# A start offset per stage for the weight tiles that TensorE reads

## The chip, the cores and the metric

The kernel runs on 1 core of a Trainium2 chip. The metric is the device time of one execution in microseconds (us). The median of three runs of the kernel before is 1837.48 us (1835.64 to 1839.0).

## The reference

Two blocks follow each other on a sequence of 256 positions and 1024 channels, in float32. The first is a mixer of four branches (a gated linear recurrence, mean pools, a chunked linear attention, a short convolution), each branch projected and gated, then an MLP. The second block runs twice: a SwiGLU layer, a mixer of windowed attention and a wide depthwise convolution, and a second SwiGLU layer. What matters here are the large products, all of the form activation times weight:

```python
proj = jnp.einsum("btd,dp->btp", u, w_in[l])            # first block, 1024 -> 6656
hid = jnp.square(jax.nn.relu(jnp.einsum("btd,df->btf", u, w_up[l])))
m = jnp.einsum("btf,fd->btd", hid, w_down[l])
...
def swiglu_ffn(h, w_up, w_down):                        # second block, twice a layer, two layers
    a, b = jnp.split(h @ w_up, 2, axis=-1)
    return (jax.nn.silu(a) * b) @ w_down
...
z = h @ w_in + b_in                                     # second block's mixer
return (g_attn * y_attn + g_conv * y_conv) @ w_out
```

## The kernel before

Activations lie transposed, channels on the 128 partitions and the 256 positions along the free dimension. TensorE multiplies in fp32r, and each factor is split in two so that the product is accurate: a value is a high part (rounded to fp32r) and a low part (the rest). A product of a weight block and an activation block is three TensorE products into the same PSUM tile: high by high, high by low, low by high.

**The weights** come in pieces of 128 x 2048 floats (1 MB), 290 of them, in the order of a queue that `plan` fills. `weights` (lines 164 to 193) handles one piece: SyncE starts a DMA into a tile `raw` (a ring of two), ScalarE casts it into a tile `hi`, and then either VectorE subtracts `hi` from `raw` into a tile `lo` (`how == 0`), or, for half of the `qkv` pieces and all `gat` pieces (`how == 1`), ScalarE writes minus the high part to `lo` and a DMA from GpSimd's queue adds the weights on top. `hi` and `lo` are rings of three tiles of 8,192 bytes per partition. `self.ahead` keeps up to two pieces prepared ahead of the one in use.

**The products.** `mm_pair` (line 225) runs a piece: for 8 blocks `k` and 2 output halves `m` three products, 48 in all, each with a 128 x 128 block of the weights as the loaded (stationary) operand and 256 columns of activations as the streamed (moving) operand:

```python
three = [(h, H), (h, L), (lo, H)]
...
nc.tensor.matmul(pt[:, m], w[:, i, c], x[k], ...)
```

`mm_duo` (line 248) does the same for two pieces at once, and lines 669 to 673 for the attention's projection. In the `qkv` stage (lines 512 to 514) the operands change places: the activations are loaded, and 512 columns of weights are streamed. Here a product means one such load of 128 columns with the stream that follows it.

**The stages**, by the names of their weights in the queue, with pieces x products of a piece: `win` 26 x 48, `wbr` 4 x 48, `wout` 4 x 48, `wup` 16 x 48, `wdown` 16 x 48, and then for each layer 0 and 1 `ffn1u` 1056 products, `ffn1d` 528, `glu` 384, `qkv` 432 (of 512 columns), `gat` 384, `att` 96, `cpr` 192, `out` 192, `ffn2u` 1056, `ffn2d` 528.

**Where the operands lie.** Pools follow each other in SBUF: `raw`, `hi`, `lo`, small constants, then the activations. In the built program the three `hi` tiles start at bytes 32,896, 41,088 and 49,280 of a partition, the `lo` tiles at 57,472, 65,664 and 73,856. These are 128 bytes past a multiple of 256. The activations that TensorE reads with them are the tiles `xs0` to `xs3` (from 99,488) and `slot0` to `slot16` (from 115,872), each in a place of 4,096 bytes, and all of them start 160 bytes past a multiple of 256. A block of weights is a multiple of 512 bytes into its tile, a block of activations a multiple of 1,024. So in every fp32r product of the kernel the weights' address less the activations' is -32 modulo 256, in all stages alike.

The instruction order is what the tile framework makes of the program order, with a few stretches raised in priority; the change touches none of it.

Of the kernel before, what the change touches and what calls it, by code (L numbers as in the profile page):

```python
# [11 lines left out]
F32R = mybir.dt.float32r  # L12
# [5 lines left out]
P = 128  # L18
# [9 lines left out]
NL = 2  # L28
NEG = -1e30
CH = 2048  # L30

PERM = np.arange(NT).reshape(16, 4, 4).transpose(2, 1, 0).reshape(-1)

# [7 lines left out]
def _pairs(w):  # L41

    k, m = w.shape
    return w.reshape(k // P, P, m // 256, 256).transpose(2, 1, 0, 3).reshape(m // 256, P, -1)


def _duo(w):

    k, m2 = w.shape
    n = m2 // 256  # L50
    return w.reshape(k // P, P, 2, n, P).transpose(3, 1, 0, 2, 4).reshape(n, P, -1)


def _wide(w):

    k, m = w.shape
    return w.reshape(k // 512, 4, P, m // 512, 512).transpose(3, 0, 2, 1, 4).reshape(
        m // 512, k // 512, P, CH)

# [15 lines left out]
def layout2(A):  # L75

    W, prm = {}, Pack()
    for l in range(NL):
# [4 lines left out]
        wi = g("w_in")  # L83
        W[f"qkv{l}"] = _wide(wi[:, :4608]).reshape(18, P, CH)
        W[f"glu{l}"] = _duo(wi[:, 4608:6656])
        W[f"gat{l}"] = _duo(wi[:, 6656:])
        W[f"att{l}"] = _wide(g("w_attn_proj")).reshape(2, P, CH)
        W[f"cpr{l}"] = _pairs(g("w_conv_proj"))
# [40 lines left out]
class Builder:  # L129
# [27 lines left out]

    def plan(self, name, i, cols=CH, c0=0, how=0):

        self.queue.append((name, i, c0, cols, how))  # L160

    def weights(self, name, i, c0=0, first=None):
        key = (name, i, c0)
        while key not in self.ready or self.next_ < min(self.ready[key][2] + 1 + self.ahead, len(self.queue)):
            n, ii, cc, w, how = self.queue[self.next_]
            nc = self.nc
            r = self.p_raw.tile([P, CH], F32, name="raw")
            h = self.p_hi.tile([P, CH], F32R, name="hi")
            lo = self.p_lo.tile([P, CH], F32R, name="lo")
            if self.next_ < 2:  # L170
                for j in range(4):
                    c = slice(j * 512, (j + 1) * 512)
                    if self.next_ == 0:
                        first(j)
                    nc.sync.dma_start(r[:, c], self.d[n][ii, :, c])
                    nc.scalar.copy(h[:, c], r[:, c])  # L176
                    nc.vector.tensor_sub(lo[:, c], r[:, c], h[:, c].bitcast(F32))
                self.ready[n, ii, cc] = (h, lo, self.next_)
                self.next_ += 1
                continue  # L180
            nc.sync.dma_start(r[:, :w], self.d[n][ii, :, cc:cc + w])
            if how == 1:
                nc.scalar.mul(lo[:, :w], r[:, :w], -1.0)  # L183
                nc.gpsimd.dma_start(lo[:, :w], self.d[n][ii, :, cc:cc + w], accum_op=ALU.add)
            nc.scalar.copy(h[:, :w], r[:, :w])  # L185
            if how == 0:
                nc.vector.tensor_sub(lo[:, :w], r[:, :w], h[:, :w].bitcast(F32))  # L187
            self.ready[n, ii, cc] = (h, lo, self.next_)
            self.next_ += 1
        h, lo, _ = self.ready[key]  # L190
        return h, lo
# [1053 lines left out]
```

## Time and profile before

| what | value |
|---|---|
| median of three runs | 1837.48 us (1835.64 to 1839.0) |
| profiled execution, its own time | 1843.05 us |
| its span, first to last instruction | 1840.9 us |
| mean granted TensorE clock | 0.988 |
| TensorE busy with products | 1774.8 us (96%), 14048 products |
| VectorE / ScalarE busy | 1328.8 us (72%) / 921.1 us (50%) |
| share of the span on the chain that ended last | TensorE 68%, DMA 10%, VectorE 10%, ScalarE 5% |

The profile page gives busy times per engine, the chain of work that ended last, and groups of instructions by source line. Products overlap one another on TensorE (one lasts 280 ns, but the next begins some 117 ns after it), so a product's duration does not say what it costs: its pace, the time from one start to the next, does. A pace is read by counting the products in a stretch in which the engine never idles.

### The profile page before, as it was taken

The numbers are of one execution on the slowest core, as the hardware profiler recorded it, in microseconds if no ns is written. First come the engines' busy times: TensorE is split into PE (matmuls) and PEld (weight loads), VectorE is DVE, ScalarE is ACT, GpSimd is POOL, SyncE is SP. The second block draws the span as 40 slices with busy tenths as digits, with TensorE's granted clock in tenths as the row PEclk, the third lists the DMA queues.
The fourth block names the chain that finished last, engine by engine and source line by source line (L and its number), as shares of the span: only waits on it lengthen the run. The fifth ranks groups of instructions, "written<-read, shape, count | busy, mean of one in ns | idle before, by whom it ended". The sixth has DMA issues, their size and how long they took to land.

```text
span 1840.9 us, 32917 instructions
## 1 busy us (share of the span) xinstructions
PE 1774.8 (96%) x14048; PEld 1693.8 (92%) x14048; DVE 1328.8 (72%) x2038; ACT 921.1 (50%) x1041; POOL 45.7 (2%) x69
## 2 busy tenths in 40 slices
PE   8999989998999999989999999999999989999997
PEld 7989889998999987778999999999997778999997
DVE  7986877546665698978776656765698988776653
ACT  5354454434444455466654445444455566654442
POOL 0000000000100000000000000100000000000000
PEclk9999999999999999989999999999999999999998
DMA  7526445554555579886455545555569986455552
GB/s 286 168 97 218 161 139 192 184 194 139 193 184 181 186 226 252 268 211 170 141 184 192 194 168 199 191 184 180 188 199 279 256 229 175 138 183 185 187 184 86
DMA packets 53570, 348.47 MB, mean 189 GB/s; under 512 B 6192, under 2 KB 6320, under 8 KB 14256
## 3 DMA queue, kind: packets, MB, share of 16 engines
q1 hardware_dynamic: 47376, 308.66, 47.4%
q0 software_dynamic: 4896, 35.65, 10.3%
q8 instruction: 110, 1.80, 0.4%
q10 hardware_dynamic: 1152, 2.06, 0.3%
q14 instruction: 36, 0.29, 0.0%
HBM read 345.30 MB, written 1.05 MB: 188 GB/s over the span
## 4 chain that ended last, share of the span: by engine, by line
PE 68%; DMA 10%; DVE 10%; ACT 5%; issue 4%; POOL 0%; ACTq 0%; DVEq 0%; POOLq 0%
PE mm L225 60%; DMA raw<-qkv 5%; DVE lo L187 4%; ACT hi L185 3%; DMA raw<-gat 2%; PE y L596 1%; DMA lo<-qkv 1%; PE mm L248 1%; PE tr L588 1%; PE pc L316 1%; PE pc L306 1%; PE sc L571 1%; DMA raw<-win 1%; DMA raw<-out 1%; PE mm L513 0%
## 5 line engine op out<-in xcount | busy, mean ns | idle before, releaser
L225 PE MATMUL mm<-xs,hi 128*128 128x256 f32 x5440 | 967.8, 282 | 10.6 <-ACT hi L176 5.9
L225 PEld LDWEIGHTS mm<-xs,hi 128*128 128x128 f32 x5440 | 825.9, 189 | 18.4 <-ACT hi L176 5.9
L187 DVE TENSOR_TENSOR lo<-raw,hi 128x2048 fp32r<-128x2048 f32 (+1 forms) x254 | 574.0, 2260 | 317.2 <-ACT hi L185 316.3
L185 ACT CAST hi<-raw 128x2048 fp32r<-128x2048 f32 (+1 forms) x288 | 541.9, 1885 | 422.8 <-PE mm L225 343.1
L225 PE MATMUL mm<-xs,lo 128*128 128x256 f32 x2720 | 739.1, 282 | 7.4 <-DVE lo L187 3.7
L225 PEld LDWEIGHTS mm<-xs,lo 128*128 128x128 f32 x2720 | 501.6, 189 | 11.6 <-DVE lo L187 4.5
L225 PE MATMUL mm<-slot,hi 128*128 128x256 f32 x2304 | 401.3, 280 | 3.0 <-DVE slot L939 2.4
L225 PEld LDWEIGHTS mm<-slot,hi 128*128 128x128 f32 x2304 | 346.1, 188 | 4.0 <-DVE slot L939 2.8
L225 PE MATMUL mm<-slot,lo 128*128 128x256 f32 x1152 | 307.6, 279 | 0.0
L225 PEld LDWEIGHTS mm<-slot,lo 128*128 128x128 f32 x1152 | 210.2, 188 | 0.0
L633 DVE SCALAR_TENSOR_TENSOR slot<-slot,prm,slot 128x256 f32<-128x256 f32 x360 | 149.2, 480 | 0.0
L340 ACT CAST slot<-f 128x256 fp32r<-128x256 f32 (+1 forms) x104 | 45.2, 439 | 196.2 <-DVE f L428 193.0
L513 PE MATMUL mm<-lo,xs 128*128 128x512 f32 x288 | 117.8, 409 | 14.5 <-DMA lo<-qkv 14.4
L514 PE MATMUL mm<-hi,xs 128*128 128x512 f32 x288 | 115.8, 402 | 0.0
L512 PE MATMUL mm<-hi,xs 128*128 128x512 f32 x288 | 115.8, 402 | 0.0
L183 ACT ACTIVATE lo<-raw 128x2048 fp32r<-128x2048 f32 x34 | 65.0, 1912 | 79.5 <-DMA raw<-qkv 55.2
L513 PEld LDWEIGHTS mm<-lo,xs 128*128 128x128 f32 x288 | 55.0, 191 | 32.7 <-DMA lo<-qkv 20.6
L341 DVE TENSOR_TENSOR slot<-f,slot 128x256 fp32r<-128x256 f32 (+1 forms) x104 | 49.0, 475 | 38.1 <-ACT slot L340 38.1
L422 DVE TENSOR_TENSOR z<-mm,rb 128x512 f32<-128x512 f32 x88 | 60.4, 690 | 11.7 <-ACT rb L334 2.5
L512 PEld LDWEIGHTS mm<-hi,xs 128*128 128x128 f32 x288 | 54.7, 190 | 12.9
L514 PEld LDWEIGHTS mm<-hi,xs 128*128 128x128 f32 x288 | 55.0, 191 | 12.4
L633 DVE SCALAR_TENSOR_TENSOR spare<-slot,prm,spare 128x256 f32<-128x256 f32 x120 | 50.0, 480 | 0.0
(272 smaller groups left out, 1299.1 us busy)
## 6 DMA issues: line engine op xcount, KB each, us to landing
raw<-ffn1u SPq DMA_DIRECT2D x44, 1024.0 KB, 4.8
raw<-ffn2u SPq DMA_DIRECT2D x44, 1024.0 KB, 4.8
raw<-qkv SPq DMA_DIRECT2D x36, 1024.0 KB, 7.7
raw<-win SPq DMA_DIRECT2D x24, 1024.0 KB, 4.8
lo<-qkv POOLq DMA_DIRECT2D x18, 1024.0 KB, 9.0
raw<-wup SPq DMA_DIRECT2D x16, 1024.0 KB, 4.8
raw<-wdown SPq DMA_DIRECT2D x16, 1024.0 KB, 4.8
raw<-ffn1d SPq DMA_DIRECT2D x16, 1024.0 KB, 4.8
```

The lines of the kernel that those rows point to most:

```text
L183: nc.scalar.mul(lo[:, :w], r[:, :w], -1.0)
L185: nc.scalar.copy(h[:, :w], r[:, :w])
L187: nc.vector.tensor_sub(lo[:, :w], r[:, :w], h[:, :w].bitcast(F32))
L225: nc.tensor.matmul(pt[:, m], w[:, i, c], x[k], start=first and m == 0 and i == 0 and j == 0, stop=last and i == n - 1 and j == 2, skip_gro ...
L248: nc.tensor.matmul(pts[e][:, m], wt[:, k, m * P:(m + 1) * P], (H, L)[x][k], start=k == 0 and w == x == m == 0, stop=k == KD - 1 and w == 1 ...
L340: nc.scalar.copy(H, src)
L341: return nc.vector.tensor_sub(L, src, H.bitcast(F32))
L422: nc.vector.tensor_mul(z, pt, norm.rb2)
L512: nc.tensor.matmul(pz[j], H[k][:, js], h[:, w], start=k == 0, stop=False)
L513: nc.tensor.matmul(pz[j], H[k][:, js], lo[:, w], start=False, stop=False)
L514: nc.tensor.matmul(pz[j], L[k][:, js], h[:, w], start=False, stop=k == 7)
L633: nc.vector.scalar_tensor_tensor(acc[i], u, w, acc[i], op0=ALU.mult, op1=ALU.add)
```

## The change

A table `BY` gives a number of bytes to 14 stages (`qkv`, `glu` and `gat` for both layers alike; `wbr`, `wout`, `att`, `cpr` and `out` are not in it and get 0). The tiles `hi` and `lo` become 64 floats (256 bytes) longer, and the weights are written, and later read, from that number of bytes after the tile's start.

```diff
+BY = {"win": 240, "wup": 224, "wdown": 240, "ffn1u0": 208, "ffn1d0": 224, "glu": 192, "gat": 192, "qkv": 32,
+      "ffn2u0": 192, "ffn2d0": 208, "ffn1u1": 176, "ffn1d1": 192, "ffn2u1": 160, "ffn2d1": 176}
...
-            h = self.p_hi.tile([P, CH], F32R, name="hi")
-            lo = self.p_lo.tile([P, CH], F32R, name="lo")
+            by = BY.get(n, BY.get(n[:-1], 0)) // 4
+            h = self.p_hi.tile([P, CH + 64], F32R, name="hi")[:, by:by + CH]
+            lo = self.p_lo.tile([P, CH + 64], F32R, name="lo")[:, by:by + CH]
```

In the program built from it every engine has the same instructions in the same order as before. The `hi` tiles start at 32,896, 41,344 and 49,792, the `lo` tiles at 58,240, 66,688 and 75,136, still 128 past a multiple of 256, and the activations move up by 1,536 bytes and keep their 160. The weights' address less the activations', modulo 256, which was -32 (that is 224) everywhere, becomes:

| stages | modulo 256 |
|---|---|
| `wbr`, `wout`, `att`, `cpr`, `out` | 224, as before |
| `win`, `wdown` | 208 |
| `wup`, `ffn1d0` | 192 |
| `ffn1u0`, `ffn2d0` | 176 |
| `glu`, `gat`, `ffn2u0`, `ffn1d1` | 160 |
| `ffn1u1`, `ffn2d1` | 144 |
| `ffn2u1` | 128 |
| `qkv` | 0 |

## Rows read from the trace of the kernel before

**Rows 1.** The page: span and busy time of each engine.
```profile
span 1840.9 us, 32917 instructions
PE 1774.8 (96%) x14048; PEld 1693.8 (92%) x14048; DVE 1328.8 (72%) x2038; ACT 921.1 (50%) x1041; POOL 45.7 (2%) x69
```

**Rows 2.** The page: shares of the chain that ended last, by engine and by line.
```profile
PE 68%; DMA 10%; DVE 10%; ACT 5%; issue 4%; POOL 0%; ACTq 0%; DVEq 0%; POOLq 0%
PE mm L225 60%; DMA raw<-qkv 5%; DVE lo L187 4%; ACT hi L185 3%; DMA raw<-gat 2%; PE y L596 1%; DMA lo<-qkv 1%; PE mm L248 1%; PE tr L588 1%; PE pc L316 1%; PE pc L306 1%; PE sc L571 1%; DMA raw<-win 1%; DMA raw<-out 1%; PE mm L513 0%
```

**Rows 3.** The chain in order of time, longest pieces: start us, us, what.
```profile
264.54 141.66 PE mm L225 x1212
456.24 174.58 PE mm L225 x1480
...
731.91 9.43 DMA raw<-qkv
...
957.15 181.77 PE mm L225 x1558
...
1648.70 167.01 PE mm L225 x1418
```

**Rows 4.** Stretches of line 225: from:to, us, engines' busy us (x count), granted clock, DMA.
```profile
core 0: us, PE busy (x) PEld busy (x), PEclk, DMA share, GB/s
340.00:400.00 60.00, 60.00 (x517) 60.00 (x516) 1.00 0.53 183
470.00:550.00 80.00, 80.00 (x682) 80.00 (x681) 1.00 0.56 193
570.00:620.00 50.00, 50.00 (x427) 50.00 (x426) 1.00 0.54 186
980.00:1060.00 80.00, 80.00 (x688) 80.00 (x687) 1.00 0.53 185
1080.00:1130.00 50.00, 50.00 (x431) 50.00 (x430) 1.00 0.53 177
1170.00:1250.00 80.00, 80.00 (x688) 80.00 (x688) 1.00 0.55 186
1660.00:1740.00 80.00, 80.00 (x682) 80.00 (x681) 1.00 0.54 186
```

**Rows 5.** Timeline of TensorE, 742.77 to 746.27 us: start us, us, instruction.
```profile
742.77 0.40 PE L513 MATMUL mm<-lo,xs 128*128 128x512 f32 x1
743.00 0.40 PE L514 MATMUL mm<-hi,xs 128*128 128x512 f32 x1
...
746.27 0.40 PE L513 MATMUL mm<-lo,xs 128*128 128x512 f32 x1
```

**Rows 6.** Timeline of TensorE, 256 us: eight products of one streamed column.
```profile
256.31 0.95 PE L306 MATMUL pc<-ones,sqa 128*128 128x1 f32 x8
257.12 0.48 PE L225 MATMUL mm<-xs,hi 128*128 128x256 f32 x2
```

**Rows 7.** Who waited for whom: total us, times, longest us.
```profile
ACT hi L185 <- PE mm L225: 343.1, 179, 8.8
DVE lo L187 <- ACT hi L185: 316.3, 189, 4.5
```

**Rows 8.** The page: weight preparation, by line.
```profile
L187 DVE TENSOR_TENSOR lo<-raw,hi 128x2048 fp32r<-128x2048 f32 (+1 forms) x254 | 574.0, 2260 | 317.2 <-ACT hi L185 316.3
L185 ACT CAST hi<-raw 128x2048 fp32r<-128x2048 f32 (+1 forms) x288 | 541.9, 1885 | 422.8 <-PE mm L225 343.1
```

**Rows 9.** The page: DMA issues of the `qkv` weights, KB each, us to landing.
```profile
raw<-qkv SPq DMA_DIRECT2D x36, 1024.0 KB, 7.7
lo<-qkv POOLq DMA_DIRECT2D x18, 1024.0 KB, 9.0
```

## The prediction

> **What bounds the kernel now.** I read the page's busy times first, then the chain, then the pace of the products inside the stretches that the chain names. TensorE is busy for 96% of the span of 1840.9 us [rows 1], and the chain that ended last lies 60% on line 225 alone, against 10% each on DMA and VectorE [rows 2]. In order of time that share comes in long unbroken pieces, 142 to 182 us each, in the up and down projections; between them, around 732 us, it lies on the transfers of the `qkv` weights [rows 3]. So a change of the products' pace goes into the time nearly in full in the projections, and little in `qkv`.
>
> The reader should now look at the pace. In stretches where TensorE never idles, the same code at the full granted clock (1.00, which is 2.4 GHz) shows two of them: 688 products in 80 us at 980 and 1170 us, but 682 at 470 and 1660 us; 431 in 50 us at 1080 us, but 427 at 570 us [rows 4]. Each count holds about two products that were already running when the stretch began. That makes 80/686 = 116.6 ns and 80/680 = 117.6 ns. The slow stretches lie in `ffn1u0`, `ffn1d0` and `ffn2u1`, the fast ones in `wdown`, `ffn2u0`, `ffn2d0` and `ffn1u1`; I count `ffn2d1`, which follows a slow stretch, as slow. The distance of the operands is the same in all of them, so something else chose between the two paces there, presumably the moment at which each stretch was resumed. Both paces are above what streaming needs: 256 columns at 2.4 GHz are 106.7 ns. The 512-column products of `qkv` start 15 times in the 3.50 us between the first and the last of the rows shown, every 233 ns, 20 ns more than the 213.3 of 512 columns [rows 5]. The excess doubles with the columns streamed. Whatever it is, it belongs to the stream and not to the weight load, which is 128 columns in both.
>
> **The change part by part.** No instruction is added, removed or reordered on any engine; addresses alone move.
>
> *Pace of the offset products.* The table covers 10,656 of the 12,000 256-column products: 1,248 in `win`, 1,536 in `wup` and `wdown`, 6,336 in the two layers' up and down projections, 1,536 in `glu` and `gat`. On the path are 60% of 1840.9 us, that is 1105 us, or some 9,400 products at 117 ns [rows 2]; less the 1,152 that line 225 runs without an offset, about 8,300. One nanosecond of pace is therefore worth 8.3 us. No row shows an fp32r product at another distance, so the price has to be bounded. Below, the bound is the array's 106.7 ns: -10 ns, -83 us. The nearest row on weight loads agrees with a floor there: eight products of a single streamed column take 0.81 us from the first start to the next group, 101 ns each [rows 6]. Above, I take the only excess that a row shows and let it occur twice: +10 ns, +83 us. Within these I stay near the fast pace that four stretches share to a tenth of a nanosecond. I take it that the four slow stages (2 x (1,056 + 528) = 3,168 products) go to 116.6 ns, which is 3,168 x 1.0 ns = 3.2 us, and that the other distances give half a nanosecond, 8,300 x 0.5 = 4.2 us.
>
> *What a rule says of this.* The rows show one distance and two paces, so they do not decide whether the distance matters. The Trainium skill (SBUF — State Buffer, "SBUF: two separate sides") says that TensorE never waits on anyone at SBUF, and that it has a second, independent read port for loading weights. By that rule the sum would be zero. The excess of 10 ns per 256 columns is not explained by it, which is why I keep it as a rival and not as the forecast.
>
> *`qkv`.* 864 products at 233 ns could gain up to 20 ns each, 17 us in all, were they on the path. They are not: the chain there is made of transfers of 8 to 10 us [rows 3, 9]. I take 0; the bounds are -17 us, and +17 us by the same doubling.
>
> *Weight preparation.* VectorE reads `raw` and `hi` at another relative offset and writes `lo` (2,260 ns each), ScalarE writes `hi` (1,885 ns) [rows 8]. If either took a tenth longer, VectorE would be busy 57 us more over the whole kernel, beside products: ScalarE's casts wait 343.1 us in total for TensorE to free a tile, VectorE's subtractions 316.3 us for those casts [rows 7]. That is the cover, and I take 0. Were it gone, the piece after next would be late by 0.2 us a piece. The 18 adding transfers of `qkv`, 9.0 us each [rows 9], now start 32 bytes later in their tiles; a tenth of the chain's 1% on them would be 2 us either way, and I take 0. The 1,536 bytes of SBUF cost no time.
>
> *The sum.* 1843.05 us of the profiled execution less 3.2 less 4.2 is 1835.7. That execution lay 5.6 us above the median of the three runs, so against the median I forecast **1830 us**.
>
> **The rivals.**
>
> *The distance does nothing* (the table does not do what it says). For it: two paces at one distance show that timing alone can choose the pace, and the rule above. Against it: an excess that grows with the stream looks like reads in each other's way. The time stays at 1837. Even so the stages could fall into the two paces in another way. All fast is -3.2 us; with the other large stages also slow (another 3,168 in the projections and 1,536 in `wup` and `wdown`) it is +4.7 us. So 1834 to 1842.
>
> *Reads that meet more often: slower.* Three stages get a distance that is a multiple of 64 bytes where the old one was not, `wup` and `ffn1d0` (192) and `ffn2u1` (128). If the load of the next weights and the stream of the current activations then run through the same places of SBUF in step, the excess of 10 ns there doubles: 768 + 528 + 1,056 = 2,352 products x 10 ns = 23.5 us, giving 1861. It decides from an average of 0.45 ns over the 8,300 products on, where 3.7 us are lost. For it: the new distances differ from each other, so they cannot all be good ones. Against it: the old distance is one point of the same unknown curve.
>
> *The excess mostly goes: much faster.* If the new distances halve it, 8,300 x 5 ns = 41 us go, and the time is 1796. For it: the floor of 107 ns. Against it: in hundreds of microseconds with different relative timing no stretch shows a pace under 116.6 [rows 4], and near 112 ns the weight preparation's cover would begin to shrink.
>
> **How the numbers follow.** A measurement of this kernel can tell about 0.2%, 3.7 us, from no change. Chances: the forecast, a modest gain, 0.33; much faster 0.09; nothing 0.26; slower 0.32. So faster by over 0.2%: 0.42; within 0.2%: 0.26; slower: 0.32. The likeliest case is the forecast at 1830, its own range 1815 to 1834. The range reaches from the halved excess to the doubled one in three stages, 1796 to 1862, and leaves out the deeper ends of both bounds.
>
> **What the profile after would show.** Counting products in stretches without idle time, stage by stage: right, if the four slow stages show 686 or more starts in 80 us and the others about 689 (116.1 ns). The group on line 225 keeps its 282 ns, since ends are modelled; it is the count that must move. The busy times of VectorE and ScalarE stay within a few microseconds. The forecast is wrong if the stages without an offset and those with one keep the same two paces (then the distance does nothing), or if some stages show paces above 118 ns (then the new distances are worse there, and which stages they are tells which distance).

## The result and the profile after

The changed kernel takes 1853.89 us (median of 5 runs, 1846.1 to 1854.11) against 1839.0 us (5 runs, 1835.64 to 1842.16) for the kernel before: a ratio of 1.0072, 95% interval 1.0048 to 1.0096. It is slower by 0.7%. The time lies inside the range of 1796 to 1862, on the other side of no change from the forecast of 1830. The profiled execution took 1854.11 us, its span 11.1 us longer than that of [rows 1].

The page of the kernel after: span, busy times, shares of the chain that ended last, weight preparation. Three lines were added to the file above line 168 and one inside `weights`, so line 225 is now 229, 187 is 191 and 185 is 189.

```profile
span 1852.0 us, 32917 instructions
PE 1781.2 (96%) x14048; PEld 1705.5 (92%) x14048; DVE 1330.0 (72%) x2038; ACT 919.5 (50%) x1041; POOL 45.7 (2%) x69
PE 70%; issue 8%; DVE 8%; DMA 7%; ACT 4%; POOL 0%; DVEq 0%; ACTq 0%; POOLq 0%
L191 DVE TENSOR_TENSOR lo<-raw,hi 128x2048 fp32r<-128x2048 f32 (+1 forms) x254 | 574.2, 2260 | 316.8 <-ACT hi L189 315.7
L189 ACT CAST hi<-raw 128x2048 fp32r<-128x2048 f32 (+1 forms) x288 | 541.0, 1881 | 437.5 <-PE mm L229 358.0
```

VectorE's subtraction still takes 2260 ns and ScalarE's cast 1881 ns against 1885 [rows 8]; the preparation of the weights was not touched. TensorE gained 6.4 us of busy time, VectorE and ScalarE changed by a microsecond or two. The view of waits says the same from the other side: ScalarE waits 14.9 us more for TensorE to free a weight tile than in [rows 7], and VectorE waits for ScalarE as before.

```profile
ACT hi L189 <- PE mm L229: 358.0, 182, 8.7
DVE lo L191 <- ACT hi L189: 315.7, 191, 4.5
```

Where the time went is seen in the pace. These are stretches of line 229 in the kernel after (from:to, us, engines' busy us with counts, granted clock, DMA), which answer to [rows 4]:

```profile
core 0: us, PE busy (x) PEld busy (x), PEclk, DMA share, GB/s
280.00:330.00 50.00, 50.00 (x427) 50.00 (x426) 1.00 0.54 183
350.00:400.00 50.00, 50.00 (x431) 50.00 (x430) 1.00 0.55 190
470.00:550.00 80.00, 80.00 (x680) 80.00 (x679) 1.00 0.55 191
980.00:1050.00 70.00, 70.00 (x586) 70.00 (x585) 1.00 0.54 183
1090.00:1115.00 25.00, 25.00 (x214) 25.00 (x213) 1.00 0.56 192
1280.00:1298.00 18.00, 18.00 (x153) 18.00 (x152) 1.00 0.46 161
1665.00:1735.00 70.00, 70.00 (x592) 70.00 (x591) 1.00 0.53 182
```

Each count holds about two products that were already running when the stretch began. At 980 us (`ffn2u0`, distance 160) that leaves 584 in 70 us, 119.9 ns each; [rows 4] give 686 in 80 us there, 116.6 ns. At 1280 us (`ffn1d1`, 160) it is 151 in 18 us, 119 ns, and at 1665 us (`ffn2u1`, 128) 590 in 70 us, 118.6. `wdown` at 350 us (208) keeps 116.6. From here on a pace is the mean of the intervals from one product's start to the next, taken over all uninterrupted products of a stage in the trace; it agrees with these counts and is finer. Where the pace changed within a stage, this mean lies between two paces.

Stage by stage, from its first to its last product, the two profiled executions differ as follows. Outside `gat`, the three distances 160, 144 and 128 cost 12.3 us together: `ffn2u0` +3.33, `ffn1u1` +3.15, `ffn1d1` +1.76, `glu` +1.05 in each layer, `ffn2d1` +1.09, `ffn2u1` +0.89. The other offsets of weights that are loaded (`win`, `wup`, `ffn1u0`, `ffn2d0`) cost 3.4 us; `qkv` (-2.0 in the two layers) and `gat` (-2.4) are shorter. In neither can that be put down to the pace: `gat` went from 116.9 to 119.7 ns a product, and `qkv` with the same offset took no less time in `e8_qkv_alone` than before (116.5 and 116.8 us in the two layers against 116.9 and 115.9). The sum is 11.3 us, against a span longer by 11.1.

### The profile page after: what moved, and what is told of

The parts are those of the page before. It is cut to its first block, busy times and chain, and to the rows that moved or that the text cites. A ratio compares the mean times of both kernels' runs of the same rounds, so it can differ in the third digit from the quotient of the medians.

```text
span 1852.0 us, 32917 instructions
## 1 busy us (share of the span) xinstructions
PE 1781.2 (96%) x14048; PEld 1705.5 (92%) x14048; DVE 1330.0 (72%) x2038; ACT 919.5 (50%) x1041; POOL 45.7 (2%) x69
## 3 DMA queue, kind: packets, MB, share of 16 engines
HBM read 345.30 MB, written 1.05 MB: 187 GB/s over the span
## 4 chain that ended last, share of the span: by engine, by line
PE 70%; issue 8%; DVE 8%; DMA 7%; ACT 4%; POOL 0%; DVEq 0%; ACTq 0%; POOLq 0%
PE mm L229 63%; DMA raw<-qkv 3%; DVE lo L191 3%; ACT hi L189 3%; DMA raw<-gat 2%; PE mm L252 1%; PE y L600 1%; PE tr L592 1%; PE pc L320 1%; PE pc L310 1%; DMA raw<-win 1%; PE sc L575 1%; DMA raw<-out 1%; DMA lo<-qkv 0%; PE pb L332 0%
## 5 line engine op out<-in xcount | busy, mean ns | idle before, releaser
L229 PE MATMUL mm<-xs,hi 128*128 128x256 f32 x5440 | 978.9, 283 | 10.3 <-ACT hi L180 6.0
L191 DVE TENSOR_TENSOR lo<-raw,hi 128x2048 fp32r<-128x2048 f32 (+1 forms) x254 | 574.2, 2260 | 316.8 <-ACT hi L189 315.7
L189 ACT CAST hi<-raw 128x2048 fp32r<-128x2048 f32 (+1 forms) x288 | 541.0, 1881 | 437.5 <-PE mm L229 358.0
L518 PE MATMUL mm<-hi,xs 128*128 128x512 f32 x288 | 113.8, 395 | 0.0
L516 PE MATMUL mm<-hi,xs 128*128 128x512 f32 x288 | 113.3, 393 | 0.0
```

The source lines that it names most:

```text
L229: nc.tensor.matmul(pt[:, m], w[:, i, c], x[k], start=first and m == 0 and i == 0 and j == 0, stop=last and i == n - 1 and j == 2, skip_gro ...
L516: nc.tensor.matmul(pz[j], H[k][:, js], h[:, w], start=k == 0, stop=False)
L518: nc.tensor.matmul(pz[j], L[k][:, js], h[:, w], start=False, stop=k == 7)
```

## The experiments

In all of them the arithmetic is that of the reference; only addresses differ. Below, a distance is the weights' address less the activations', modulo 256, as in the table ahead of the prediction: 224 plus the bytes in `BY`. The edits are against the changed kernel; each replaces the two lines of its table, which are shown as removed in the first only, and long tables are broken or cut.

**1. The room alone: `e1_pad_only`.**

```diff
-BY = {"win": 240, "wup": 224, "wdown": 240, "ffn1u0": 208, "ffn1d0": 224, "glu": 192, "gat": 192, "qkv": 32,
-      "ffn2u0": 192, "ffn2d0": 208, "ffn1u1": 176, "ffn1d1": 192, "ffn2u1": 160, "ffn2d1": 176}
+BY = {}
```

> The tiles keep their 256 bytes more, and the table is empty: every offset is 0 and every distance is 224 modulo 256 again. If the distance sets the pace, the dense stages go back to 116.7 ns (686 starts in 80 us), some perhaps to 117.8, and the time to that of the kernel before, 1836 to 1842 us. If the longer tiles or the moved activations cost the time, it stays near 1854 us and the up and down projections stay near 120 ns.

Measured: 1839.78 us, ratio to the kernel before 0.9989 (0.9978 to 1.0). The longer tiles and the activations moved up by 1,536 bytes cost nothing; the loss is in the offsets. The stretches of this kernel showed again the two paces of [rows 4], in other stages than before: `ffn1u0` at 470 us now has 688 in 80 us, and `wup` 427 in 50 us. So which of the two paces a stage has is not a property of the stage.

```profile
280.00:330.00 50.00, 50.00 (x427) 50.00 (x426) 1.00 0.54 182
470.00:550.00 80.00, 80.00 (x688) 80.00 (x687) 1.00 0.54 191
```

**2. Weights and activations moved together: `e4_shift_both`.** Every weight tile starts 192 bytes later, and so do the activations, so the distance stays 224.

```diff
+BY = {'win': 192, 'wbr': 192,
...
+      'ffn2u1': 192, 'ffn2d1': 192}
-        self.eps = self.con.tile([P, 16], F32, name="eps")
+        self.eps = self.con.tile([P, 64], F32, name="eps")
```

> All weights start 192 bytes into their tiles, and the activations are moved up by 192 bytes too (a larger constant tile ahead of them), so that each address differs from the kernel before and the distance is 224 modulo 256 again in all stages. If the distance sets the pace, all dense stages run at 116.7 or 117.8 ns, and the time is 1836 to 1842 us. If it is the weights' own start (64 past a multiple of 256, as it was in the stages at 120 ns), they run at 120 ns and the time is above 1855 us.

One execution: 1840.92 us. In stretches at 980 and 1160 us, which ran at distances 160 and 144 in the changed kernel, the old pace is back: 601 products in 70 us, 116.5 ns. An offset of 192 bytes, the one that made `ffn2u0` and `ffn1d1` slow, does nothing when the activations move with it. It is the distance that counts.

```profile
980.00:1050.00 70.00, 70.00 (x603) 70.00 (x602) 1.00 0.52 182
1160.00:1230.00 70.00, 70.00 (x602) 70.00 (x601) 1.00 0.56 198
```

**3. The slow distances undone: `e9_undo_far`.** The offsets that give 192, 176, 208 and `qkv`'s 0 stay; those that give 160, 144 and 128 are taken back to 224.

```diff
+BY = {'win': 240, 'wup': 224, 'wdown': 240, 'ffn1u0': 208, 'ffn1d0': 224, 'qkv': 32, 'ffn2d0': 208}
```

> The change with the offsets of the stages at the distances 160, 144 and 128 taken out (glu, gat, ffn2u0, ffn1u1, ffn1d1, ffn2u1, ffn2d1 back to 224); the rest of the table stays. If the loss is those stages' pace, 768 products in glu, 2,112 in ffn2u0 and ffn1u1 and 1,056 in ffn1d1 and ffn2d1 go from 120.0 to 116.7 ns, and 1,056 in ffn2u1 from 118.7 to 116.7: 3,936 x 3.3 + 1,056 x 2.0 = 15 us, so 1838 to 1841 us against 1853.9 and within 0.2% of the kernel before. If something that all offsets share costs it, half of the loss or more stays, 1846 us or above.

Measured: 1841.61 us, ratio 0.9995 (0.998 to 1.001). The loss is gone, so it lay in the stages at 160, 144 and 128.

**4. `qkv` alone: `e8_qkv_alone`.**

```diff
+BY = {'qkv': 32}
```

> Only qkv keeps its offset of 32 bytes (distance 0); all other stages are at 224. If the distance sets the pace, qkv's 864 products run at 227.6 ns in place of 233.3, which is 4.9 us were all of them on the path; its stage in the changed kernel gained -0.4 us in layer 0 and 2.4 us in layer 1, so I expect 1 to 4 us less than the kernel before, and no difference at all if the transfers alone bound the stage. The other stages show 116.7 or 117.8 ns.

Measured: 1841.06 us, ratio 0.9995 (0.998 to 1.0009). The pace of the 512-column products falls from 233.2 to 227.6 ns. The gain of 1 to 4 us that was expected does not show; the interval reaches from 3.7 us less to 1.7 us more, so a small gain is not excluded. That the transfers bound that stage [rows 3] is the likely reason.

**5. Two ladders of distances.** Ten of the large stages and the two `qkv` stages are each a probe of a distance of its own, so that one execution reads twelve.

```diff
+BY = {'wup': 16, 'wdown': 32, 'ffn1u0': 48, 'ffn1d0': 64, 'ffn2u0': 80, 'ffn2d0': 96, 'ffn1u1': 112, 'ffn1d1': 128, 'ffn2u1': 144, 'ffn2d1': 0, 'qkv0': 16, 'qkv1': 48}
```

> Ten dense stages get ten offsets not tried yet: wup 16, wdown 32, ffn1u0 48, ffn1d0 64, ffn2u0 80, ffn2d0 96, ffn1u1 112, ffn1d1 128, ffn2u1 144, ffn2d1 0 bytes, which are the distances 240, 0, 16, 32, 48, 64, 80, 96, 112 and 224 modulo 256; qkv0 gets 16 (240), qkv1 48 (16). If the distance sets the pace, each stage has one pace of its own, ffn2d1 has 116.7, and the values run on from the known ones: about 116.7 at 240 next to 224, and above 117 at 96 and 112 next to the 118.7 at 128. If only the moment of resuming a stretch chose between 116.7 and 117.8, all ten show one of these two.

```diff
+BY = {'wup': 144, 'wdown': 112, 'ffn1u0': 80, 'ffn1d0': 48, 'ffn2u0': 16, 'ffn2d0': 128, 'ffn1u1': 96, 'ffn1d1': 64, 'ffn2u1': 32, 'ffn2d1': 240, 'qkv0': 96, 'qkv1': 192}
```

> The same distances given to other stages: wup 144, wdown 112, ffn1u0 80, ffn1d0 48, ffn2u0 16, ffn2d0 128, ffn1u1 96, ffn1d1 64, ffn2u1 32, ffn2d1 240 bytes (distances 112, 80, 48, 16, 240, 96, 64, 32, 0 and 208); qkv0 gets 96 (64), qkv1 192 (160). If the distance sets the pace, each distance shows the pace it had in the ladder before to 0.2 ns, whatever stage carries it, and ffn2d1 at 208 shows the 116.7 of win and wdown in the changed kernel. If the stage or its place in time sets it, the paces stay with the stages instead.

One execution each: 1845.06 us (low) and 1855.79 us (mixed). The stretches of the low ladder at 350 (`wdown`, distance 0), 1090 (`ffn2d0`, 64) and 1665 us (`ffn2u1`, 112):

```profile
350.00:400.00 50.00, 50.00 (x419) 50.00 (x418) 1.00 0.54 188
1090.00:1115.00 25.00, 25.00 (x223) 25.00 (x223) 1.00 0.61 207
1665.00:1735.00 70.00, 70.00 (x586) 70.00 (x585) 1.00 0.53 187
```

Distance 64 has 221 products in 25 us, 113.1 ns, where the same stage had 212, counted alike, at 176 in the changed kernel. Distance 0 has 119.9. The mixed ladder puts other distances on the same stages, at 470 (`ffn1u0`, 48), 980 (`ffn2u0`, 240) and 1665 us (`ffn2u1`, 0):

```profile
470.00:550.00 80.00, 80.00 (x651) 80.00 (x650) 1.00 0.51 178
980.00:1050.00 70.00, 70.00 (x586) 70.00 (x585) 1.00 0.53 183
1665.00:1735.00 70.00, 70.00 (x586) 70.00 (x585) 1.00 0.52 183
```

All distances that are multiples of 16, mean pace in ns, over the changed kernel and the runs above; two values where two stages or executions differed:

| distance | pace | distance | pace |
|---|---|---|---|
| 0 | 120.0 | 128 | 118.7 |
| 16 | 118.3 | 144 | 120.0 |
| 32 | 118.3 | 160 | 120.0 |
| 48 | 118.0, 122.7 | 176 | 118.1 |
| 64 | 113.4, 113.6 | 192 | 117.8 |
| 80 | 118.8, 119.1 | 208 | 116.7, 118.0 |
| 96 | 117.3, 118.7 | 224 | 116.7, 117.8 |
| 112 | 120.0 | 240 | 117.6, 120.0 |

The pace goes with the distance: 0, 16, 32 and 112 were each read on two stages and agreed to 0.1 ns. At 48, 96 and 240 there are two paces at one distance, as at 224 before, so the forecast that a distance shows the same pace to 0.2 ns on any stage failed there. Some entries are means of two paces that follow each other within a stage: 122.7 at 48 is 117.8 and then 123.3, and 118.0 at 208 is 116.7 and then 120.0. The old distance is, with 208, the next best of the sixteen; 64 alone is clearly better.

**6. One distance for all: `e5_all_64`.** All weights that are loaded get 96 bytes, `qkv` 32.

```diff
+BY = {'win': 96, 'wbr': 96,
...
+      'qkv1': 32, 'gat1': 96, 'att1': 96, 'cpr1': 96, 'out1': 96, 'ffn2u1': 96, 'ffn2d1': 96}
```

> All stages start 96 bytes into their tiles, the distance 64 that ran at 113.4 to 113.6 ns in both ladders; qkv starts at 32, the distance 0 of the change. If the distance sets the pace, every dense stage shows about 113.5 ns, 3.2 ns less than 116.7; over the 9,400 products on the path that is 30 us, so 1807 to 1813 us against 1841. If the weights' preparation or their transfers become the bound at the faster pace, stretches without idle time vanish and less than half of it comes, above 1825 us.

Measured: 1818.61 us, ratio 0.9879 (0.9859 to 0.99), 22.7 us faster than the kernel before. That is more than the 1807 to 1813 us that were expected. Most long stretches of the profiled execution hold 113.3 to 113.6 ns; `glu`, `att` and `cpr` of layer 1 and the last pieces of `wdown` had a second pace of 117 to 118. That execution was one of the two fastest of the six, at 1812.61 us; what the slower ones lost is not shown.

**7. Finer steps.** Ten distances in steps of 4 bytes around 64, and ten elsewhere:

```diff
+BY = {'wup': 84, 'wdown': 88, 'ffn1u0': 92, 'ffn1d0': 100, 'ffn2u0': 104, 'ffn2d0': 108, 'ffn1u1': 72, 'ffn1d1': 120, 'ffn2u1': 136, 'ffn2d1': 96}
```

> Offsets that are multiples of 4 or 8 bytes around the best one: wup 84, wdown 88, ffn1u0 92, ffn1d0 100, ffn2u0 104, ffn2d0 108, ffn1u1 72, ffn1d1 120, ffn2u1 136 bytes (distances 52, 56, 60, 68, 72, 76, 40, 88, 104 modulo 256), ffn2d1 96 (64). If the pace follows steps of 16 bytes, each shows the pace of a multiple of 16 beside it; if it follows the distance byte by byte, the paces lie between 113.4 at 64 and 118 to 119 at 48 and 80, and 60 and 68 are the fastest of them or faster than 64. VectorE's subtraction into tiles that start at an odd word (84, 92, 100, 108) may take longer than its 2.3 us.

```diff
+BY = {'wup': 228, 'wdown': 232, 'ffn1u0': 236, 'ffn1d0': 244, 'ffn2u0': 248, 'ffn2d0': 252, 'ffn1u1': 4, 'ffn1d1': 12, 'ffn2u1': 44, 'ffn2d1': 40}
```

> Ten more distances in steps of 4 bytes: wup 196, wdown 200, ffn1u0 204, ffn1d0 212, ffn2u0 216, ffn2d0 220, ffn1u1 228, ffn1d1 236, ffn2u1 12, ffn2d1 8 modulo 256. The three distances that ran near 113.4 ns, 52, 64 and 76, lie 12 bytes apart, the ones between them at 118 to 119.5. If fast distances recur every 12 bytes (so also at 196 and 220, and at 4 and 232), those at 196 and 220 show 113.4 ns and their neighbours 200, 212 and 216 do not. If the neighbourhood of 64 is special, all ten lie between 116 and 120 ns.

One execution each, 1845.4 and 1849.95 us. The first: 52 at 113.8 ns, 56 at 117.8, 60 at 119.5, 68 and 72 at 118.3, 76 at 113.4, and 40, 88, 104 at 119.2, 116.7, 117.9. So 52, 64 and 76 were fast and 56, 60, 68 and 72 between them slow, against the expectation that 60 and 68 would be among the fastest or show the pace of a multiple of 16. The three are 12 bytes apart, and the second run asked whether that goes on: 196, 200, 216, 220, 228 and 236 took 118.3 to 120.7 ns, 204 took 114.4, 212, 12 and 8 took 117.3, 116.7 and 115.6. A recurrence every 12 bytes would have shown 196 and 220 at 113.4 ns; they took 118.3 and 120.7. The other forecast, that all ten lie between 116 and 120, fails at 204, 8 and 220. Each of the slow distances was read on one stage in one execution, and a distance can have two paces: the 119.2 at 200 is 120.0 and 116.7 in two stretches. So a fast pace that did not occur here is not excluded for the slow ones. No rule for the fast distances was found.

**8. The two other fast distances everywhere: `e11_all_52` and `e12_all_76`.** As experiment 6, with 84 and 108 bytes for 96.

```diff
+BY = {'win': 84, 'wbr': 84,
...
+      'qkv1': 32, 'gat1': 84, 'att1': 84, 'cpr1': 84, 'out1': 84, 'ffn2u1': 84, 'ffn2d1': 84}
```

> All stages at the distance 52 (qkv at 0). In one stage it ran at 113.8 ns. At the distance 64 some stages ran at 117.8 in place of 113.3 ns; if that second pace belongs to the distance 64, the time here is below 1816 us, with all dense stages at 113.3 to 113.8. If every fast distance has such a second pace, it is 1812 to 1824 us, like that at 64. Tiles start at an odd word; VectorE's subtraction should stay at 2.29 us.

```diff
+BY = {'win': 108, 'wbr': 108,
...
+      'qkv1': 32, 'gat1': 108, 'att1': 108, 'cpr1': 108, 'out1': 108, 'ffn2u1': 108, 'ffn2d1': 108}
```

> All stages at the distance 76 (qkv at 0). In one stage it ran at 113.4 ns. If the second pace of 117.8 ns belongs to the distance 64 alone, all dense stages show 113.4 and the time is below 1816 us; if every fast distance has it, 1812 to 1824 us.

Measured: 1819.99 us, ratio 0.9863 (0.9836 to 0.9891), and 1814.71 us, ratio 0.9852 (0.9822 to 0.9881). Their intervals overlap. At distance 52 `ffn2u0` fell to a second pace of 120.0 ns, the stretch at 980 us here, while `ffn1u1` at 1160 us ran at 113.3:

```profile
980.00:1050.00 70.00, 70.00 (x585) 70.00 (x585) 1.00 0.52 181
1160.00:1230.00 70.00, 70.00 (x620) 70.00 (x619) 1.00 0.57 198
```

At 76 all the up and down projections from `wdown` on are fast. The second half of `win` ran at 120.0 ns, so this distance too has a second pace. The page, the waits and five stretches; the first two are `win`, before and after a pause of TensorE at 126 us:

```profile
span 1812.9 us, 32917 instructions
PE 1736.0 (96%) x14048; PEld 1658.7 (91%) x14048; DVE 1322.9 (73%) x2038; ACT 920.6 (51%) x1041; POOL 45.8 (3%) x69
```

```profile
ACT hi L188 <- PE mm L228: 316.1, 179, 9.2
DVE lo L190 <- ACT hi L188: 298.9, 192, 5.0
```

```profile
40.00:60.00 20.00, 20.00 (x179) 20.00 (x178) 1.00 0.62 224
140.00:180.00 40.00, 40.00 (x336) 40.00 (x335) 1.00 0.60 211
470.00:550.00 80.00, 80.00 (x708) 80.00 (x707) 1.00 0.57 197
980.00:1050.00 70.00, 70.00 (x620) 70.00 (x619) 1.00 0.56 196
1665.00:1735.00 70.00, 70.00 (x620) 70.00 (x619) 1.00 0.55 192
```

TensorE loses 38.8 us of busy time against [rows 1] with the same 14,048 products, and ScalarE's wait for a free tile shrinks from 343.1 to 316.1 us, so the cover of the weight preparation is nearly whole. This version beats both kernels. Its time is below the 1816 us that were expected if the second pace belonged to the distance 64 alone. The traces speak against that reason all the same: each of the three fast distances showed a second pace.

The traces also show when a pace is chosen. In all fifteen there are 255 stretches of 145 products or more of one stage without a pause or another product between them. After the first 48 products the mean over 48 stays the same to 0.5 ns until the stretch ends, in every one. The pace changes where TensorE has been interrupted. At 224, 97 of 142 such stretches (of 100 products or more) ran at 116.7 ns and 45 at 117.8; at 64, 52 and 76 together, 60 of 68 ran at 113.3 and the rest at 117.7 to 120.0.

**9. Which of the two reads is in the way.** A product's interval can be long because of its own weights, or because the next product's weights are loaded while it streams. In a group of three, two products with a high part are followed by one with a low part. If high and low lie at different distances, the three kinds of interval tell the two cases apart.

```diff
+BY = {'win': 96, 'wbr': 96,
...
+            bl = by if n[:3] == "qkv" else 48
...
-            lo = self.p_lo.tile([P, CH + 64], F32R, name="lo")[:, by:by + CH]
+            lo = self.p_lo.tile([P, CH + 64], F32R, name="lo")[:, bl:bl + CH]
```

Here the high parts lie at 64, the low parts at 160 (48 floats).

> The high parts lie at distance 64 (113.4 ns where all three products had it), the low parts at 160 (120 ns), in all stages but qkv, which is left at 224. The three products are high by high, high by low, low by high. If the load of the next weights meets the running stream, the product before the low one (whose stream runs while the low part is loaded) is the slow one of the three; if a product's own load and stream meet, it is the low one itself. In both cases the mean of the three is near (2 x 113.4 + 120)/3 = 115.6 ns. If the mean is 120 or 113.4, one of the two distances decides alone.

The same with the two turned round:

```diff
+BY = {'win': 192, 'wbr': 192,
...
+            bl = by if n[:3] == "qkv" else 24
```

> The split of distances turned round: the high parts lie at distance 160, the low parts at 64 (qkv as before). In the split with the high parts at 64 and the low parts at 160, the interval that ended with the start of a low product was 122.7 ns, the other two kinds 115.2 to 116.2. Theory (the load of the next weights meets the stream that is running, so the distance of the next weights decides): now both kinds of interval that end with the start of a high product are long (120 to 123 ns) and the one from a high to a low product is short (113 to 116 ns); mean pace of a stage about 120 ns, time about 1865 us. Rival one (the interval from a high to a low product is long whatever the distances): it stays at 122 to 123 ns, the others at 115 to 116. Rival two (the distance of the product that runs decides): the intervals that begin with a high product are long, both of them, and the one that begins with a low product is short.

One execution each: 1856.55 and 1855.69 us. The intervals are read from the starts in the timeline of TensorE, here of the first split (start us, us, instruction):

```profile
1199.78 0.40 PE L229 MATMUL mm<-xs,hi 128*128 128x256 f32 x2
1200.02 0.28 PE L229 MATMUL mm<-xs,lo 128*128 128x256 f32 x1
1200.14 0.40 PE L229 MATMUL mm<-xs,hi 128*128 128x256 f32 x2
1200.37 0.28 PE L229 MATMUL mm<-xs,lo 128*128 128x256 f32 x1
```

From the start of the first high product to that of the low one are 0.24 us, from there to the next high one 0.12. The rows are rounded to 10 ns; the trace itself has single nanoseconds, and each kind has some 330 intervals or more. Mean interval by kind in ns, `ffn1u1`; the last column is `e5_all_64`, where both lie at 64:

| runs now, then loaded next | high 64, low 160 | high 160, low 64 | both 64 |
|---|---|---|---|
| high, then high | 115.2 | 119.0 | 114.1 |
| high, then low | 122.8 | 116.2 | 113.4 |
| low, then high | 116.2 | 119.1 | 113.5 |

In both splits the intervals into weights at 160 are long and those into weights at 64 short, whichever product runs. In the first two rows of a column the product that runs has its weights at the same distance, yet the second is 7.6 ns longer in the one split and 2.8 ns shorter in the other. That leaves neither the running product's own distance nor the step from high to low as the cause. `wdown`, `ffn1d1` and `ffn2u1` show the same signs. So it is the distance of the weights to be loaded next that makes an interval long or short. That their load meets the stream that is running is the nearest explanation, but no row shows the meeting itself: a weight load is recorded at 188 ns in `e12_all_76` and 190 ns in the changed kernel in this stage. One group does not fit. Once in each of the 22 pieces, before the last block, where the order of the three products turns round, a low product follows a low one; the mean there was 118.2 ns into 160 and 119.5 into 64. The sizes are not settled either. The first split was forecast at a mean of 115.6 ns and came to 118.0; the second was forecast at about 120 ns a product and 1865 us, and came to 118.2 in this stage and 1855.7 in all. A mixture is not the mean of its parts.

## Why the prediction was right or wrong

**What bounds the kernel: right.** A nanosecond of pace was to be worth 8.3 us. In the changed kernel the mean over the 10,656 offset products rose by 1.6 ns (117.1 to 118.7), which at that price is 13 us; the span grew by 11.1. At distance 76 all 12,000 products moved, for which the same sum gives 9.4 us a nanosecond: the mean fell by 3.2 ns (to 113.9), 30 us, and the median by 26.8 us (1841.48 to 1814.71). So the price is somewhat too high, and the path is right. The bounds of 106.7 and 127 ns held every stage: 113.3 to 122.7.

**The terms taken as nothing: right.** Room, weight preparation and `qkv` cost nothing that the runs can tell (`e1_pad_only`, the page after, `e8_qkv_alone`). The products of `qkv` did become faster, by 5.6 ns each, and no gain in time shows, as argued. The 18 adding transfers were not tried by themselves.

**"The other distances give half a nanosecond": wrong, and this is the step that failed.** Of the two terms of the sum it was the one without a row, and it was kept near the fast pace that four stretches share. Those stretches are all at 224 and said nothing of other distances. The term gave 4.2 us back; the runs show a loss in its place. 3,936 products (`ffn2u0`, `ffn1u1`, `ffn1d1`, `ffn2d1`, `glu` twice) went to 120.0 ns, 2.2 to 3.3 above what they had, and 1,056 (`ffn2u1`) to 118.7. At 3.3 and 0.9 ns that is at most 14 us, of which 12.3 show; the median lost 14.9.

**"The four slow stages go to 116.6": wrong.** `ffn1u0` went to 118.1, `ffn1d0` stayed at 117.8, `ffn2u1` and `ffn2d1` became slower. A stage may have either pace at distance 224 without any change, as `e1_pad_only` showed. The guess that the moment of resuming a stretch chooses between them is borne out by the stretches in experiment 8, in that a pace changes only at an interruption.

**The rival "slower": the right side, in part the right mechanism, the wrong places.** It named the load of the next weights against the stream, and a multiple of 64 bytes as the point where they fall in step. The multiples of 64 are 0 (120.0), 64 (113.4, the fastest), 128 (118.7) and 192 (117.8); the slowest stages of the change were at 160 and 144. Of the three stages that it named, `ffn2u1` lost 0.9 ns, `wup` 1.1 and `ffn1d0` nothing, where it had 10 ns each. It gave 1861, 7 us above the result, and that nearness is luck.

**"It belongs to the stream and not to the weight load": wrong.** The excess that doubles with the columns was read as one that the weight load can't cause, since that is 128 columns in both. The two splits of experiment 9 show that the distance of the weights to be loaded moves it. What is left of it at the fast distances, 113.3 against 106.7 ns, no run takes apart.

**The rule against which the sum was weighed.** The measurements contradict the zero that was drawn from it: with the order of the instructions unchanged and at the full granted clock, the pace of `ffn1u1` went from 113.4 ns (at 76) to 120.0 (at 144) by addresses alone, and experiment 9 puts it down to the weights to be loaded next. The Trainium skill (SBUF — State Buffer, "SBUF: two separate sides") has TensorE never wait on anyone at SBUF and load weights through an independent read port; for fp32r products of this form the runs do not bear out that the pace is then free of where the operands lie, and the measurement decides. The rival of 1834 to 1842 built on it was wrong with it.

**The rival "much faster"** was not what this table does, but its claim that part of the excess of 10 ns can go is true: the fast stretches of `e5_all_64`, `e11_all_52` and `e12_all_76`, at 113.3 ns, are a third of it below 116.7. Half of it, near 112 ns, was not reached by any distance tried.

## What to carry to other kernels

Where TensorE bounds a kernel, count its starts in an uninterrupted stretch before changing anything else: the pace is a quantity of its own, and here the distance between the loaded and the streamed operand moved it from 116.7 ns down to 113.3 and up to 120.0 and more. A distance can't be chosen by reasoning from one known point; give each stage of one build its own, read many in one execution, and then set one good distance everywhere. Read each distance in more than one uninterrupted stretch, and time the winner more than once, because one distance can show two paces.

## What was not expected of the hardware

- The pace differed between distances 4 bytes apart: 113.4 ns at 76 and 118.3 at 72, 113.4 to 113.6 at 64 and 119.5 at 60, with 72 and 60 read on one stage each. It is periodic enough in 256 that the three tiles of a ring, which lie an odd multiple of 256 apart in the built program, show one pace within a stage.
- One distance can have two paces, in stretches of one execution: 116.7 and 117.8 at 224, 113.3 and 120.0 at 52 and at 76. A pace holds until TensorE is interrupted, and another can follow. What chooses was not found. It also limits how well a distance can be read from one execution.
- VectorE took no notice of tiles that begin 84 bytes into their place: 2296 ns a subtraction in `e11_all_52`, 2294 in the kernel before.
- Open: why 52, 64, 76 and 204 are fast, and whether a faster distance exists. Of the 64 distances in steps of 4 bytes, 29 were not tried.
